# Hybrid mLSTM and convolution layer on Trainium2: readout joined to its gate, nine staging tiles for the w_out operands, and other slots at the start and the end

## Chip, core and metric

One core of one Trainium2 chip. The metric is the device time of one execution in microseconds: 1683.57 is the median of three runs of the kernel before (1682.82 to 1685.95).

## The reference

All in float32, 2048 tokens (S), width 1024.

```
h   = RMSNorm(x)                              # x: (2048, 1024)
P   = h @ w_in                                # 1024 x 8200: q k v o z_m i f | u B C z_c
y_m = silu(z_m) * sigmoid(o) * HeadNorm(mLSTM(q, k, v, i, f))   # 4 heads, dqk 128, dv 256
y_c = silu(z_c) * GroupNorm(B * causal_conv3(C * u))            # 16 groups of 64 channels
out = x + RMSNorm(concat(y_m, y_c) @ w_out)   # w_out: 2048 x 1024
```

The mLSTM is a chunkwise recurrence with a running-maximum stabiliser; in the kernel a chunk is 128 tokens and a group is two chunks of one head.

## The kernel before

**Products.** A matrix product of 256 by 1024 by 1024 (a *pair* of 128 columns each, times 1024 tokens) is done as seven products of quarters instead of eight (sums of quarters of both operands, a Winograd form). Each quarter product is 12 matmuls of 128x128 by 128x512, because each float32 operand is split into a high part and a rest (`split_h` on ScalarE, L190; `split_l` on VectorE, L193) and three of the four part products are kept (`mm_prod`, L309 to L311). The seven products use three PSUM banks in the order X D Y X Y D Y; `evac(j)` empties or copies a bank after product j, and TensorE may go on in that bank only then. The tile c that `evac(4)` makes (L532, VectorE) has to be done before product 6, the copy u of `evac(2)` (L527, ScalarE) before product 4.

**Passes and slots.** Pass 0 is the first 1024 tokens times w_in (32 pairs), pass 1 the second 1024 tokens (32 pairs); passes 2 and 3 are w_out (8 pairs each): first the half of its rows that takes y of the convolution, with the sums stored in DRAM (c_scr), then the half that takes the mLSTM's, added to them. One quarter product is one *slot*; U = 224 slots are a pass over w_in. Slots 0 to 13 are a start without the seven-product form (`start`), slots 14 to 27 do pairs 2 and 3 in turns (`two_pairs`); slot 224 begins pass 1, 448 pass 2, 504 pass 3. The order of everything is written out by hand: `on(slot, fn)` and `later(d, fn)` put work on an agenda, and `run_slot` emits a slot's entries in the order evacuations, weights, stores, all else. `in_order` then ties each engine to that order, SyncE included, which issues all DMAs. So an instruction that waits holds up everything behind it on its engine.

**Weights.** For the product of slot s, the loads are at s-8, the sums of quarters at s-5 (`w_sum`), the high part at s-4 and the rest at s-3.

**Operands of a pass.** Each of the seven operands (128 x 4 x 512) is loaded in two halves, m = 0 to 13 (`hop_fill`), into one of four staging tiles of 128x1024 (tags cv, cv, cu, rb, which other helpers use too), then split (`hop_high` at slot end-6+11m/14, `hop_low` a slot later) into tiles that the pass before has left product by product. The loads are put at end-10 for m < 4, and two slots after the staging tile's former user for the others.

**Pairs of a pass over w_in.** Pairs 0 to 7 give q, k and v, 8 to 23 the convolution, 24 to 31 the gates o and z_m (`take_oz`; `gate_oz`, L358 to L364, three slots after). `gate_oz` stores the gate to g_scr. The 32 groups of the mLSTM (`plan_group`) start every 10.4 slots in pass 0 and every 10.8 in pass 1, the last at slot 422, and store their readout h to h_scr at start+15. `o_make` (L1212) loads h and gate of one tile of 128 tokens, multiplies them, and stores to o_scr, where pass 3 reads: for the first 1024 tokens every 10 slots in pass 1, for the second every 4 slots from slot 452, in pass 2 and the first slots of pass 3.

**Start.** Squares of x, `inverse`, `diagonal` and `spread` give the norm's factors of one 512 tokens; `norm`, `diff` and `fill` make the operands of pass 0. v of head 0 is taken in slots 22 to 25 (`slow` in `plain_take`); its transpose on VectorE follows a slot later and four stores to v_scr of 64 KB each a slot after that.

**Pools.** Tag t5 has ten tiles of 128x512 for all that is short-lived; the mLSTM's tiles are in the pool `ml`, closed after pass 1, and the last pool, `op`, takes its place.

**End.** `row_take` adds c_scr's part to a tile of the result, squares it, and two slots after both halves of a row are there `row_out` scales it and adds x.

Of the kernel before, what the change touches and what calls it, by code (L numbers as in the profile page):

```python
# [9 lines left out]
F32 = mybir.dt.float32  # L10
F32R = mybir.dt.float32r
AF = mybir.ActivationFunctionType
ALU = mybir.AluOpType
# [52 lines left out]
def hybrid_layer_kernel(  # L66
# [39 lines left out]
    def scratch(name, shape):  # L106
        return [dram.tile(shape, F32, name=f"{name}{i}") for i in range(2)]

    y_scr = scratch("y_scr", [8, P, HT])
    h_scr = scratch("h_scr", [NH, NC, 2, P, P])  # L110
    g_scr = scratch("g_scr", [8, P, HT])
# [68 lines left out]
    def c4(tag, name, shape=None, dtype=F32):  # L180
        return cpool.tile(shape or [P, HT], dtype, tag=tag, name=name, bufs=2 if tag == "cv" else 1)
# [54 lines left out]

    def y_quarter(pas, t, half):

        src = (y_scr, o_scr)[pas][t // NC]
# [76 lines left out]
    def seg(qd):  # L316
        return slice(Q * qd, Q * qd + Q)
# [32 lines left out]
    def take_oz(hf, e, ch, qd, src, psum):  # L350
        if ch == 0:
            S["so", qd] = sigmoid(src)
        else:
            def go():
                S["z", qd] = (src, sigmoid(src))
            later(1, go)
            later(3, lambda: gate_oz(hf, e, qd))

    def gate_oz(hf, e, qd):
        so = S.pop(("so", qd))  # L360
        z, sz = S.pop(("z", qd))
        nc.vector.scalar_tensor_tensor(z, z, gh[:, e : e + 1], so, ALU.mult, ALU.mult)
        nc.vector.tensor_tensor(z, z, sz, ALU.mult)
        store(g_scr[hf][e][:, seg(qd)], z)  # L364

    def take_uc(hf, j, ch, qd, src, psum):
        if (ch, qd) == (0, 0):
# [77 lines left out]
    def gate_zz(hf, g, ch, qd, src, sg):  # L445
        cv = S["cv", ch][:, seg(qd)]
        nc.vector.tensor_tensor(sg, src, sg, ALU.mult)
        nc.vector.tensor_tensor(sg, sg, cv, ALU.mult)
        store(y_scr[hf][2 * g + ch][:, seg(qd)], sg)

    TAKE = {"qk": take_qk, "v": take_v, "oz": take_oz, "uc": take_uc, "bb": take_bb, "zz": take_zz}

# [7 lines left out]

    def row_take(n, ch, qd, src, psum):
        t = 2 * n + ch
        last = n == NOUT - 1 and ch == 0
        o = S["ot", t, qd] = op.tile([P, Q], F32, tag="ot", name="ot", bufs=4)
        nc.vector.tensor_tensor(o, src, S.pop(("pc", ch, qd)), ALU.add)

        def square():
            ss = op.tile([P, 1], F32, tag=f"oss{qd}", name="oss")
            nc.scalar.activation(t5("junk"), o, AF.Square, accum_out=ss)
            S.setdefault(("oss", t), []).append(ss)  # L470
            if len(S["oss", t]) == 1 + (n < NOUT - 1):
                S["xr", t] = op.tile([P, DM], F32, tag="xr", name="xr")
                nc.sync.dma_start(S["xr", t], x[t * P : (t + 1) * P, :])
            if len(S["oss", t]) == 2:
                row_rstd(t, last)

        def scale():
            nc.vector.tensor_tensor(o, o, S["gpost"][:, seg(qd)], ALU.mult)  # L478

        if last and qd == 1:  # L480
            square()
            scale()
        else:
            later(1, square)
            later(2, scale)

    def row_rstd(t, last):
        a, b = S.pop(("oss", t))
        nc.vector.tensor_tensor(a, a, b, ALU.add)
        rstd(a, 1.0 / DM)  # L490
        later(0 if last else 2, lambda: row_out(t, a, last))

    def row_out(t, r, last):
        xr = S.pop(("xr", t))
        for qd in range(2):
            o, dst = S.pop(("ot", t, qd)), out[t * P : (t + 1) * P, seg(qd)]
            nc.vector.scalar_tensor_tensor(o, o, r, xr[:, seg(qd)], ALU.mult, ALU.add)  # L497
            store(dst, o, 0 if last else 1)

    TAKE_OUT = (part_store, row_take)  # L500

# [404 lines left out]
    def hop_source(pas, j):  # L906

        if pas == 1:
            return hop_scr[j]
        half, ch = {0: (0, 0), 3: (1, 0), 6: (1, 1)}.get(j, (None, None))  # L910
        if half is None:
            return wo_scr[pas - 2][j]
        r = WOUT0[pas - 2] + half * KH * P
        return wout[r : r + KH * P, seg(ch)].rearrange("(e p) c -> p e c", p=P)

    def hop_fill(pas, m):

        j, half = divmod(m, 2)
        t = c4(STAGE[m % 4], "hst", [P, 2, Q])
        ks = slice(2 * half, 2 * half + 2)  # L920
        nc.sync.dma_start(t, hop_source(pas, j)[:, ks, :])
        return j, ks, t

    def hop_high(pas, m):
        j, ks, t = S["fill", pas, m]
        if m % 2 == 0:
            hops[pas, j] = (hop_tile(j, "H", f"hH{j}"), hop_tile(j, "L", f"hL{j}"))
        split_h(hops[pas, j][0][:, ks], t)

    def hop_low(pas, m):  # L930
        j, ks, t = S.pop(("fill", pas, m))
        H, L = hops[pas, j]
        split_l(H[:, ks], L[:, ks], t)


    def start():
# [110 lines left out]
        def plain_take(n, ch, qd, bank, t=None):  # L1047
            t = t or t5("u")
            nc.vector.tensor_tensor(t, bank, rb[:, seg(qd)], ALU.mult)
            kind, i = PAIRS[n]  # L1050
            slow = NSTART + 8 + 2 * ch + qd - clock[0] if kind == "v" else 0
            later(slow, lambda: TAKE[kind](0, i, ch, qd, t, False))

        load(0, 0)
        load_raw((0, 0, 0), wt[0, 0])
# [72 lines left out]

        p0 = [plain(0, 0, 1)]
        norm(2)  # L1130
        diagonal(1)
        fill(0, 0)
        run_slot()

        p0.append(plain(0, 1, 1))
        spread(1)
        fill(3, 2)
        spread_take(1)
        run_slot()

# [70 lines left out]

    def o_make(t, half):  # L1212

        hf, tt = divmod(t, NC)
        es, ts = slice(4 * half, 4 * half + 4), slice(tt * P, (tt + 1) * P)
        R = {}
        view = lambda a: a.rearrange("p (e t) -> p e t", t=P)

        def load():
            R["h"], R["g"] = t5("yh"), t5("yg")  # L1220
            for i in range(2):
                nc.sync.dma_start(
                    view(R["h"])[:, 2 * i : 2 * i + 2, :], h_scr[hf][2 * half + i, tt].rearrange("e p t -> p e t"))
            nc.sync.dma_start(view(R["g"]), g_scr[hf][es, :, ts].rearrange("e p t -> p e t"))

        def mult():
            nc.vector.tensor_tensor(R["h"], R["h"], R["g"], ALU.mult)
            store(o_scr[hf][es, :, ts].rearrange("e p t -> p e t"), view(R["h"]))

        return (0, load), (3, mult)  # L1230

# [13 lines left out]
    for i in range(NH * NG):  # L1245
        h, g = divmod(i, NG)
        plan_group(0, h, g, 47 + int(10.4 * i))
        plan_group(1, h, g, U + 36 + int(10.8 * i))
    for i in range(NC):
        on(60 + 10 * i, lambda i=i: norm_stat(i))  # L1250
    on(150, norm_fin)
# [1 line left out]
    for k in range(KH):  # L1253
        on(OZ0 + 10 + 9 * k, lambda k=k: hop_load(k))
        on(OZ0 + 15 + 9 * k, lambda k=k: hop_make(k))
        for p, s in enumerate((U + OZ0, 2 * U)):
            for d, fn in wo_make(p, k):
                on(s + 10 + 9 * k + d, fn)
    for i in range(2 * NT):
        for d, fn in o_make(*divmod(i, 2)):  # L1260
            on((U + 40 + 10 * i if i < NT else 2 * U + 4 + 4 * (i - NT)) + d, fn)

    def plan_fill(pas, end):
        for m in range(2 * NPROD):
            s = end - 6 + 11 * m // 14
            early = end - 10 if m < 4 else end - 6 + 11 * (m - 4) // 14 + 2
            def load(m=m):
                S["fill", pas, m] = hop_fill(pas, m)
            on(early, load)
            on(s, lambda m=m: hop_high(pas, m))  # L1270
            on(s + 1, lambda m=m: hop_low(pas, m))
# [7 lines left out]
        pair(0, n)  # L1279

    for n in range(NPAIR):
        pair(1, n)
# [4 lines left out]
    mlx.close()  # L1287


    op = ctx.enter_context(tc.tile_pool(name="op", bufs=2, reuse_waits="tile"))  # L1290
    S["gpost"] = op.tile([P, DM], F32, tag="gpost", name="gpost", bufs=1)
    nc.sync.dma_start(S["gpost"], g_post.broadcast_to([P, DM]))
# [4 lines left out]
    for pas in (2, 3):  # L1297
        for n in range(NOUT):
            pair(pas, n)
    while any(agenda.values()):  # L1300
        run_slot()

# [52 lines left out]
```

## Time and profile before

| | |
|---|---|
| median of 3 runs | 1683.57 us |
| the profiled execution | 1679.38 us, span 1677.6 us, mean granted clock 0.997 |
| TensorE, matmul | 1648.6 us busy, 98% |
| VectorE | 1276.7 us, 76% |
| ScalarE | 885.2 us, 53% |
| GpSimd | 129.5 us, 8% |
| DMA | 339 MB, 66.7% of 16 engines on SyncE's queue |

TensorE is busy throughout; the slices in which it is not are found from who waited for whom, and the instructions in order of time around the wait. Matmuls are pipelined: each is shown 0.39 us long, and they start every 0.227 us.

### The profile page before, as it was taken

The numbers are of one execution on the slowest core, as the hardware profiler recorded it, in microseconds if no ns is written. First come the engines' busy times: TensorE is split into PE (matmuls) and PEld (weight loads), VectorE is DVE, ScalarE is ACT, GpSimd is POOL, SyncE is SP. The second block draws the span as 40 slices with busy tenths as digits, with TensorE's granted clock in tenths as the row PEclk, the third lists the DMA queues.
The fourth block names the chain that finished last, engine by engine and source line by source line (L and its number), as shares of the span: only waits on it lengthen the run. The fifth ranks groups of instructions, "written<-read, shape, count | busy, mean of one in ns | idle before, by whom it ended". The sixth has DMA issues, their size and how long they took to land. (4 is left out here: it accounts for less than half of the span.)

```text
span 1677.6 us, 23360 instructions
## 1 busy us (share of the span) xinstructions
PE 1648.6 (98%) x7565; PEld 1366.9 (81%) x7565; DVE 1276.7 (76%) x2373; ACT 885.2 (53%) x1703; POOL 129.5 (8%) x142
## 2 busy tenths in 40 slices
PE   9999999999999999999999999999999999999997
PEld 7778888888888888788888888888888878887886
DVE  6987679898989788946557877786877586578886
ACT  6543456565656565634444556565565563355442
POOL 1000002010202001000000201010200000000111
PEclk9999999999999999999999999999999999999999
DMA  7378755564455688856885546455587688898764
GB/s 266 116 178 225 190 182 160 152 192 158 151 166 162 213 273 275 266 141 167 208 216 165 168 138 180 146 170 160 186 249 228 226 270 257 267 306 286 255 208 163
DMA packets 414539, 339.23 MB, mean 202 GB/s; under 512 B 191337, under 2 KB 306033, under 8 KB 414418
## 3 DMA queue, kind: packets, MB, share of 16 engines
q1 hardware_dynamic: 414418, 337.76, 66.7%
q8 instruction: 59, 0.97, 0.2%
q14 instruction: 62, 0.51, 0.1%
HBM read 218.90 MB, written 118.76 MB: 201 GB/s over the span
## 5 line engine op out<-in xcount | busy, mean ns | idle before, releaser
L190 ACT CAST w<-wraw 128x512 fp32r<-128x512 f32 x506 | 313.5, 621 | 292.0 <-PE uY L311 106.4
L193 DVE TENSOR_TENSOR w<-wraw,w 128x512 fp32r<-128x512 f32 x506 | 344.1, 684 | 104.5 <-ACT w L190 102.7
L309 PE MATMUL uY<-hH,w 128*128 128x512 f32 x936 | 368.3, 393 | 13.2 <-DVE c L532 6.3
L310 PE MATMUL uY<-hL,w 128*128 128x512 f32 x936 | 365.4, 390 | 0.0
L311 PE MATMUL uY<-hH,w 128*128 128x512 f32 x936 | 365.3, 390 | 0.0
L309 PE MATMUL uX<-hH,w 128*128 128x512 f32 x624 | 243.8, 391 | 2.2 <-ACT uY L521 2.2
L311 PE MATMUL uX<-hH,w 128*128 128x512 f32 x624 | 243.2, 390 | 1.6 <-DVE w L193 1.6
L309 PE MATMUL uD<-hH,w 128*128 128x512 f32 x624 | 244.6, 392 | 0.0
L311 PE MATMUL uD<-hH,w 128*128 128x512 f32 x624 | 243.2, 390 | 0.0
L310 PE MATMUL uD<-hL,w 128*128 128x512 f32 x624 | 243.0, 389 | 0.0
L310 PE MATMUL uX<-hL,w 128*128 128x512 f32 x624 | 242.9, 389 | 0.0
L309 PEld LDWEIGHTS uY<-hH,w 128*128 128x128 f32 x936 | 176.1, 188 | 52.7 <-DVE c L532 6.5
L311 PEld LDWEIGHTS uY<-hH,w 128*128 128x128 f32 x936 | 176.1, 188 | 37.5
L310 PEld LDWEIGHTS uY<-hL,w 128*128 128x128 f32 x936 | 176.3, 188 | 35.1 <-DVE hL L193 0.5
L309 PEld LDWEIGHTS uX<-hH,w 128*128 128x128 f32 x624 | 117.2, 188 | 26.8 <-ACT uY L521 3.0
L311 PEld LDWEIGHTS uX<-hH,w 128*128 128x128 f32 x624 | 117.1, 188 | 26.7 <-DVE w L193 2.0
L311 PEld LDWEIGHTS uD<-hH,w 128*128 128x128 f32 x624 | 117.1, 188 | 24.8
L310 PEld LDWEIGHTS uX<-hL,w 128*128 128x128 f32 x624 | 117.2, 188 | 23.7
L309 PEld LDWEIGHTS uD<-hH,w 128*128 128x128 f32 x624 | 117.2, 188 | 23.5
L310 PEld LDWEIGHTS uD<-hL,w 128*128 128x128 f32 x624 | 117.3, 188 | 23.3
L532 DVE TENSOR_TENSOR c<-p,uY 128x512 f32<-128x512 f32 x78 | 53.3, 684 | 86.3 <-PE uY L311 83.5
L527 ACT COPY u<-uY 128x512 f32<-128x512 f32 x78 | 45.6, 585 | 94.1 <-PE uY L311 92.8
(201 smaller groups left out, 2221.9 us busy)
## 6 DMA issues: line engine op xcount, KB each, us to landing
wraw<-in_wt_dram SPq DMA_DIRECT2D x226, 256.0 KB
wraw<-w_scr SPq DMA_DIRECT2D x120, 256.0 KB
w_scr<-wraw SPq DMA_DIRECT2D x90, 256.0 KB
v_scr<-tr SPq DMA_DIRECT2D x128, 64.0 KB
vraw<-v_scr SPq DMA_DIRECT2D x32, 256.0 KB
h_scr<-hT SPq DMA_DIRECT2D x128, 64.0 KB
y_scr<-sg SPq DMA_DIRECT2D x32, 256.0 KB
g_scr<-c SPq DMA_DIRECT2D x32, 256.0 KB
```

Source lines behind the costliest of these rows:

```text
L190: nc.scalar.copy(dH, src)
L193: nc.vector.tensor_tensor(dL, src, dH.bitcast(F32), ALU.subtract)
L309: nc.tensor.matmul(bank, wH[:, k, :], bH[:, k, :], start=first, stop=False, **kw)
L310: nc.tensor.matmul(bank, wH[:, k, :], bL[:, k, :], start=False, stop=False, **kw)
L311: nc.tensor.matmul(bank, wL[:, k, :], bH[:, k, :], start=False, stop=stop and k == KH - 1, **kw)
L527: nc.scalar.copy(sb["u"], bank["Y"])
L532: nc.vector.tensor_tensor(c, sb["p"], bank["Y"], ALU.add)
```

## The change

1. **Readout and gate joined for the second 1024 tokens.** `take_oz` loads the readout h from h_scr a slot after the take, and `gate_oz`, now four slots after the take, multiplies it in as a third operation and stores the product straight to o_scr. `o_make` is left for the first 1024 tokens alone, every 8 slots.
2. **Nine staging tiles for passes 2 and 3.** The pool `ml` is closed before pair 31 of pass 1, and a pool `stage` with five tiles of 128x1024 opens in its place. Loads m = 4 to 8 go to it at end-7 to end-5, m = 9 to 12 to the first four tiles at end-4 to end-2, and m = 13 goes to two tiles of t5 at end+1. `stage` closes at product 4 of pass 3, where `op` opens.
3. **y of the convolution by tiles.** y_scr is laid out so that a load of one quarter (128 x 4 x 128) is contiguous, 2 KB a partition, and the stores are in pieces of 512 B; before, the stores were contiguous and the loads in pieces of 512 B.
4. **Start.** `fill(0, 0)` and `fill(3, 2)` go ahead of `diagonal(1)`; v of head 0 is taken in slots 16, 19, 21 and 23, and the second half of k of head 0 in slot 15 instead of at once.
5. **Groups of the mLSTM** start every 10 slots or a little more, so that start modulo 7 is neither 1 nor 3: the last of pass 1 starts at slot 418 instead of 422.
6. **End.** The last pair's rows are squared and scaled at once, the odd row is finished ahead of the even one, the sum of a row's two squares moves from VectorE to GpSimd, and x is loaded a slot earlier.

```diff
-    y_scr = scratch("y_scr", [8, P, HT])
+    y_scr = scratch("y_scr", [NC, 2, P, 4, P])
...
-            later(3, lambda: gate_oz(hf, e, qd))
+            if hf == 0:
+                later(3, lambda: gate_oz(hf, e, qd))
+            else:
+                later(1, lambda: readout_load(e, qd))
+                later(4, lambda: gate_oz(hf, e, qd))
+
+    def readout_load(e, qd):
+        t = S["h", qd] = t5("yh")
+        h, dv = divmod(e, 2)
+        nc.sync.dma_start(
+            t.rearrange("p (c t) -> p c t", t=P),
+            h_scr[1][h, 4 * qd : 4 * qd + 4, dv].rearrange("c p t -> p c t"))
...
-        store(g_scr[hf][e][:, seg(qd)], z)
+        if hf:
+            nc.vector.tensor_tensor(z, z, S.pop(("h", qd)), ALU.mult)
+        store((g_scr, o_scr[1])[hf][e][:, seg(qd)], z)
...
-        store(y_scr[hf][2 * g + ch][:, seg(qd)], sg)
+        half, e = divmod(2 * g + ch, 4)
+        store(
+            y_scr[hf][4 * qd : 4 * qd + 4, half, :, e, :].rearrange("c p t -> p c t"),
+            sg.rearrange("p (c t) -> p c t", t=P))
...
+        end = n == NOUT - 1
...
+        square()
+        if full:
+            row_rstd(t)
+        scale()
+        if (ch, qd) == (0, 1):
+            row_out(t + 1)
+            row_out(t)
...
-        nc.vector.tensor_tensor(a, a, b, ALU.add)
+        nc.gpsimd.tensor_tensor(a, a, b, ALU.add)
...
-        t = c4(STAGE[m % 4], "hst", [P, 2, Q])
+        i = m % (4 if pas == 1 else 9)
...
+        if m == 13 and pas > 1:
+            parts = [(slice(k, k + 1), t5("hst")[:, None, :]) for k in (2, 3)]
+        elif i < 4:
+            parts = [(ks, c4(STAGE[i], "hst", [P, 2, Q]))]
+        else:
+            parts = [(ks, S["stage"].tile([P, 2, Q], F32, tag=f"st{i}", name="hst"))]
...
-            slow = NSTART + 8 + 2 * ch + qd - clock[0] if kind == "v" else 0
-            later(slow, lambda: TAKE[kind](0, i, ch, qd, t, False))
+            slot = {("v", 0, 0): 16, ("v", 0, 1): 19, ("v", 1, 0): 21, ("v", 1, 1): 23, ("qk", 1, 1): 15}
+            later(slot.get((kind, ch, qd), clock[0]) - clock[0], lambda: TAKE[kind](0, i, ch, qd, t, False))
...
         norm(2)
-        diagonal(1)
         fill(0, 0)
         run_slot()
 
         p0.append(plain(0, 1, 1))
+        fill(3, 2)
+        diagonal(1)
         spread(1)
-        fill(3, 2)
         spread_take(1)
...
+    for hf, first in enumerate((47, U + 36)):
+        s = first - 10
+        for i in range(NH * NG):
+            s += 10
+            while s % NPROD in (1, 3):
+                s += 1
+            plan_group(hf, *divmod(i, NG), s)
...
-    for i in range(2 * NT):
+    for i in range(2 * NC):
         for d, fn in o_make(*divmod(i, 2)):
-            on((U + 40 + 10 * i if i < NT else 2 * U + 4 + 4 * (i - NT)) + d, fn)
+            on(U + 40 + 8 * i + d, fn)
...
-            early = end - 10 if m < 4 else end - 6 + 11 * (m - 4) // 14 + 2
+            n = 4 if pas == 1 else 9
+            if m == 13 and pas > 1:
+                early = end + 1
+            elif m >= n:
+                early = end - 6 + 11 * (m - n) // 14 + 2
+            elif m < 4:
+                early = end - 11 + m // 2
+            else:
+                early = end - 7 + (m - 4) // 2
```

## Rows read from the trace of the kernel before

**Rows 1.** Waits of TensorE, 55 to 130 us: total us, times, longest

```profile
PE uY L309 <- DVE c L532: 3.0, 1, 3.0
PE uX L309 <- ACT uY L521: 2.2, 2, 1.5
PE uX L311 <- DVE w L193: 1.6, 1, 1.6
PE uY L309 <- ACT uY L521: 0.8, 1, 0.8
```

**Rows 2.** Waits of TensorE, 250 to 690 us (two rows), 720 to 1300 us (two rows)

```profile
PE uY L309 <- DVE c L532: 1.6, 1, 1.6
PE uY L309 <- ACT uY L521: 0.4, 1, 0.4
...
PE uY L309 <- ACT uY L521: 0.7, 1, 0.7
PE num L701 <- DVE pL L193: 0.7, 1, 0.7
```

**Rows 3.** TensorE in order of time: start, us, instruction, [idle before, releaser]

```profile
1351.23 0.39 PE L309 MATMUL uY<-hH,w 128*128 128x512 f32 x1
1353.95 0.39 PE L309 MATMUL uX<-hH,w 128*128 128x512 f32 x1
...
1366.70 0.50 PE L309 MATMUL uY<-hH,w 128*128 128x512 f32 x1 [1.71 <-ACT u L527]
1372.79 0.47 PE L309 MATMUL uY<-hH,w 128*128 128x512 f32 x1 [0.36 <-DVE c L532]
...
1523.34 0.79 PE L309 MATMUL uY<-hH,w 128*128 128x512 f32 x1 [3.27 <-ACT u L527]
1526.80 0.40 PE L311 MATMUL uY<-hH,w 128*128 128x512 f32 x1
...
1550.28 0.50 PE L309 MATMUL uY<-hH,w 128*128 128x512 f32 x1 [0.60 <-DVE c L532]
```

**Rows 4.** The start in order of time, VectorE, ScalarE and SyncE's queue

```profile
47.42 0.57 ACT L997 COPY rb<-ssq 128x512 f32<-128x512 f32 x1
49.84 5.39 DVE L1002 SCALAR_TENSOR_TENSOR xs<-xs,gp,rb 128x512 f32<-128x512 f32 x8
58.61 0.71 DVE L329 STREAM_TRANSPOSE tr<-u 128x512 f32<-128x512 f32 x1
...
110.48 5.68 SPq L214 DMA_DIRECT2D v_scr<-tr  x8
```

**Rows 5.** Waits of VectorE, 40 to 126 us

```profile
DVE s L251 <- DMA wraw<-in_wt_dram: 5.6, 1, 5.6
```

**Rows 6.** VectorE in order of time, ahead of slot 448

```profile
1338.97 0.69 DVE L193 TENSOR_TENSOR w<-wraw,w 128x512 fp32r<-128x512 f32 x1 [0.64 <-ACT w L190]
...
1342.19 0.74 DVE L362 SCALAR_TENSOR_TENSOR c<-c,gh,sg 128x512 f32<-128x512 f32 x1
...
1348.99 0.68 DVE L532 TENSOR_TENSOR c<-p,uY 128x512 f32<-128x512 f32 x1
```

**Rows 7.** Waits of VectorE, 1337 to 1374 us

```profile
DVE hL L193 <- ACT hH L190: 1.9, 3, 1.3
```

**Rows 8.** Waits of ScalarE, 1497 to 1528 us

```profile
ACT hH L190 <- DMA hst<-wo_scr: 7.1, 5, 4.1
```

**Rows 9.** The end in order of time, VectorE and GpSimd

```profile
1667.61 0.69 DVE L465 TENSOR_TENSOR ot<-uY,pc 128x512 f32<-128x512 f32 x1 [0.63 <-PE uY L311]
1671.82 0.93 POOL L426 TENSOR_TENSOR oss<-oss,mhalf 128x1 f32<-128x1 f32 x1
1673.04 1.41 DVE L497 SCALAR_TENSOR_TENSOR ot<-ot,oss,xr 128x512 f32<-128x512 f32 x2
```

**Rows 10.** One item of o_make after slot 452: its last load, its product

```profile
1368.57 0.47 SPq L1224 DMA_DIRECT2D yg<-g_scr  x1
1376.15 0.68 DVE L1227 TENSOR_TENSOR yh<-yh,yg 128x512 f32<-128x512 f32 x1
```

More of the change, by code (lines that the diff above doesn't have):

```diff
@@ L107, in scratch @@
         return [dram.tile(shape, F32, name=f"{name}{i}") for i in range(2)]
-    y_scr = scratch("y_scr", [8, P, HT])
+    y_scr = scratch("y_scr", [NC, 2, P, 4, P])
     h_scr = scratch("h_scr", [NH, NC, 2, P, P])
-    g_scr = scratch("g_scr", [8, P, HT])
+    g_scr = dram.tile([8, P, HT], F32, name="g_scr")
     graw_scr = scratch("graw_scr", [4, NH, HT])
@@ L237, in y_quarter @@
     def y_quarter(pas, t, half):
-        src = (y_scr, o_scr)[pas][t // NC]
+        if pas == 0:
+            return y_scr[t // NC][t % NC, half]
+        src = o_scr[t // NC]
         return src[4 * half : 4 * half + 4, :, t % NC * P : (t % NC + 1) * P].rearrange("e p t -> p e t")
@@ L462, in row_take @@
         t = 2 * n + ch
-        last = n == NOUT - 1 and ch == 0
+        end = n == NOUT - 1
         o = S["ot", t, qd] = op.tile([P, Q], F32, tag="ot", name="ot", bufs=4)
         nc.vector.tensor_tensor(o, src, S.pop(("pc", ch, qd)), ALU.add)
+        full = ("oss", t) in S
+        if not full:
+            S["oss", t] = op.tile([P, 2], F32, tag="oss", name="oss", bufs=4)
+        ss = S["oss", t][:, qd : qd + 1]
+        if full != end:
+            S["xr", t] = op.tile([P, DM], F32, tag="xr", name="xr")
+            nc.sync.dma_start(S["xr", t], x[t * P : (t + 1) * P, :])
@@ L467, in square @@
         def square():
-            ss = op.tile([P, 1], F32, tag=f"oss{qd}", name="oss")
             nc.scalar.activation(t5("junk"), o, AF.Square, accum_out=ss)
[L470 to L475, printed above, removed]
         def scale():
@@ L478, in scale @@
             nc.vector.tensor_tensor(o, o, S["gpost"][:, seg(qd)], ALU.mult)
[L480 to L483, printed above, removed]
+        if not end:
             later(1, square)
             later(2, scale)
-    def row_rstd(t, last):
-        a, b = S.pop(("oss", t))
-        nc.vector.tensor_tensor(a, a, b, ALU.add)
+            if full:
+                later(1, lambda: row_rstd(t))
+                later(3, lambda: row_out(t))
+            return
+        square()
@@ L490, in row_rstd, with row_out @@
+        if full:
+            row_rstd(t)
[3 more added lines that the diff above has]
+            row_out(t)
+    def row_rstd(t):
+        a, b = (S["oss", t][:, qd : qd + 1] for qd in range(2))
+        nc.gpsimd.tensor_tensor(a, a, b, ALU.add)
         rstd(a, 1.0 / DM)
[L491 to L495, printed above, removed]
+    def row_out(t):
+        xr, r = S.pop(("xr", t)), S.pop(("oss", t))[:, 0:1]
+        for qd in (1, 0):
@@ L496, in row_out @@
             o, dst = S.pop(("ot", t, qd)), out[t * P : (t + 1) * P, seg(qd)]
             nc.vector.scalar_tensor_tensor(o, o, r, xr[:, seg(qd)], ALU.mult, ALU.add)
-            store(dst, o, 0 if last else 1)
+            store(dst, o, 0 if t >= NT - 2 else 1)
     TAKE_OUT = (part_store, row_take)
@@ L918, in hop_fill @@
         j, half = divmod(m, 2)
-        t = c4(STAGE[m % 4], "hst", [P, 2, Q])
+        i = m % (4 if pas == 1 else 9)
         ks = slice(2 * half, 2 * half + 2)
-        nc.sync.dma_start(t, hop_source(pas, j)[:, ks, :])
-        return j, ks, t
+        if m == 13 and pas > 1:
[4 more added lines that the diff above has]
+            parts = [(ks, S["stage"].tile([P, 2, Q], F32, tag=f"st{i}", name="hst"))]
+        for ks, t in parts:
+            nc.sync.dma_start(t, hop_source(pas, j)[:, ks, :])
+        return j, parts
     def hop_high(pas, m):
-        j, ks, t = S["fill", pas, m]
+        j, parts = S["fill", pas, m]
         if m % 2 == 0:
             hops[pas, j] = (hop_tile(j, "H", f"hH{j}"), hop_tile(j, "L", f"hL{j}"))
-        split_h(hops[pas, j][0][:, ks], t)
+        for ks, t in parts:
+            split_h(hops[pas, j][0][:, ks], t)
     def hop_low(pas, m):
-        j, ks, t = S.pop(("fill", pas, m))
+        j, parts = S.pop(("fill", pas, m))
         H, L = hops[pas, j]
-        split_l(H[:, ks], L[:, ks], t)
+        for ks, t in parts:
+            split_l(H[:, ks], L[:, ks], t)
     def start():
@@ L1212, in o_make @@
     def o_make(t, half):
-        hf, tt = divmod(t, NC)
-        es, ts = slice(4 * half, 4 * half + 4), slice(tt * P, (tt + 1) * P)
+        es, ts = slice(4 * half, 4 * half + 4), slice(t * P, (t + 1) * P)
         R = {}
@@ L1222, in load @@
                 nc.sync.dma_start(
-                    view(R["h"])[:, 2 * i : 2 * i + 2, :], h_scr[hf][2 * half + i, tt].rearrange("e p t -> p e t"))
-            nc.sync.dma_start(view(R["g"]), g_scr[hf][es, :, ts].rearrange("e p t -> p e t"))
+                    view(R["h"])[:, 2 * i : 2 * i + 2, :], h_scr[0][2 * half + i, t].rearrange("e p t -> p e t"))
+            nc.sync.dma_start(view(R["g"]), g_scr[es, :, ts].rearrange("e p t -> p e t"))
         def mult():
             nc.vector.tensor_tensor(R["h"], R["h"], R["g"], ALU.mult)
-            store(o_scr[hf][es, :, ts].rearrange("e p t -> p e t"), view(R["h"]))
+            store(o_scr[0][es, :, ts].rearrange("e p t -> p e t"), view(R["h"]))
         return (0, load), (3, mult)
@@ L1244, in hybrid_layer_kernel @@
     plan_gates(1, U + 9, False)
[L1245 to L1248, printed above, removed]
+    for hf, first in enumerate((47, U + 36)):
[5 more added lines that the diff above has]
+            plan_group(hf, *divmod(i, NG), s)
     for i in range(NC):
@@ L1281, in hybrid_layer_kernel @@
     for n in range(NPAIR):
+        if n == NPAIR - 1:
+            mlx.close()
+            stx = ExitStack()
+            S["stage"] = stx.enter_context(tc.tile_pool(name="stage", bufs=1, reuse_waits="tile"))
         pair(1, n)
@@ L1286, in hybrid_layer_kernel @@
                 later(0, lambda qd=qd, bank=bank: gate_take(1, qd, bank))
[L1287 to L1292, printed above, removed]
     for n in range(NOUT):
@@ L1296, in hybrid_layer_kernel @@
             on(s + d, lambda n=n, ch=ch, qd=qd: part_load(n, ch, qd))
-    for pas in (2, 3):
-        for n in range(NOUT):
-            pair(pas, n)
+    for n in range(NOUT):
+        pair(2, n)
+    step = products(3, 0, bank_)
+    for j in range(NPROD):
+        if j == 4:
+            stx.close()
+            op = ctx.enter_context(tc.tile_pool(name="op", bufs=2, reuse_waits="tile"))
+            S["gpost"] = op.tile([P, DM], F32, tag="gpost", name="gpost", bufs=1)
+            nc.sync.dma_start(S["gpost"], g_post.broadcast_to([P, DM]))
+        step(j)
+    for n in range(1, NOUT):
+        pair(3, n)
     while any(agenda.values()):
```

## The prediction, on record before the changed kernel ran

> **What bounds the kernel now.** I read the busy table first, then TensorE's waits, then the instructions around each. TensorE is busy nearly all the time, and the change adds and removes no matmul, so only its stops and what follows the last matmul can move. From product to product the start moves by 2.72 us for 12 matmuls [rows 3], 0.227 us each. A stop costs about 0.27 us more than the idle shown: a matmul is drawn 0.39 us long, 0.16 over its pitch, and the first after a stop takes 0.11 longer. The stops are in five places:
>
> - the start: 3.0 + 2.2 + 1.6 + 0.8 = 7.6 us in five stops [rows 1], with 5 x 0.27 about 8.9;
> - the middle of passes 0 and 1: 1.6 + 0.4 + 0.7 + 0.7 in four [rows 2], about 4.5;
> - around slot 448: 1.71 and 0.36 [rows 3], about 2.6;
> - around slot 504: 3.27, then 8 pitches that take 3.46 us in place of 1.81 (1523.34 to 1526.80), then 0.60 [rows 3]: 3.43 + 1.65 + 0.87 = 5.9;
> - the end: VectorE's last operations finish 1673.04 + 1.41, some 6.9 us after the last product's bank is read at 1667.61 [rows 9].
>
> The reader is to see in rows 5 to 8 that each of these waits for VectorE or ScalarE, and that behind these stands a DMA that SyncE issued late, or VectorE's own queue.
>
> **Start, two effects.** First, `fill(0, 0)` and `fill(3, 2)` now precede the diagonal, for which ScalarE waits. Their VectorE halves then run before the factors rb are there; so `norm(1)` can start when rb is copied, at 47.42 + 0.57 = 48.0, instead of 49.84: 1.8 us. One transpose of k (0.71 in the row, some 0.65 from start to start) [rows 4] leaves the chain as well. VectorE is thus 2.4 us earlier at the first stop, which removes it (1.6 + 0.27), and leaves 0.5 for the next two. The moved transposes (k at slot 16, v at 17, 20, 22, 24 for 23 to 26) come back behind these, but their number is the same by slot 27. I take 2.4 us, between 0.7 (the transpose alone) and 4.8 (all three stops of 2.2 and 1.6).
>
> Second, the stop of 3.0: VectorE waits 5.6 us for weights [rows 5], whose load stands in SyncE's queue behind eight v_scr stores that take 5.68 us [rows 4], 0.71 each. Four of the eight are v of head 0, which now go several slots earlier: 4 x 0.71 = 2.8 us, of the 3.27 that the stop costs. Below nothing is possible if the same stores in slots 18 to 25 delay weights there; the loads are issued eight slots ahead, so I take 2.8, from 0 to 3.3. The start together: **-5.2**.
>
> **Middle.** The group's starts move by up to four slots. The stops there are single meetings of a group's operations with the convolution's, with `gate_oz` or with the sums for pass 1, on VectorE or ScalarE. Where `hop_make` (slots 183 to 186) met the transposes of a readout at 185, these now fall on 187: I count the stop of 1.6 as gone (1.9 with its share) and the three small ones as replaced by others. **-1.9**, between -4.5 and +2 (as many new ones as there were, half the size). Around slot 224 the loads keep their four tiles and nearly their slots: 0.
>
> **Slot 448.** Here the change works in both directions. Nine tiles bring the loads m = 4 to 12 three to four slots forward, so ScalarE no longer waits for them. But VectorE is nearly full, and its order is by slots: between 1337 and 1374 it waits only 1.9 us, three times [rows 7]. The change makes each `gate_oz` longer by one operation of 0.68 [rows 10], 1.4 to 2.1 us from start to start, and puts it one slot later. The two gates of pair 30 were in slots 442 and 443 and are in 443 and 444. The first one used to fill time in which VectorE waits for a cast of ScalarE anyway (the wait that ends at 1338.97); now nothing does. From 1342.19, the start of a gate, to c of pair 31 at 1348.99 [rows 6] there was one gate of 1.4 us, and there will be two of 2.1: c starts at 1348.99 + 0.7 + 2.1 = 1351.8 and ends at 1352.5, and product 6 wants its bank at 1351.23 [rows 3]. A new stop of 1.3 us. From this c to the next, the one that released 1372.79, are 1372.79 - 0.1 - 0.7 - 1348.99 = 23.0 us, with two more gates in it (+1.4) and 1.6 us of the waits of rows 7, which go: 22.8. So the next c starts at 1374.6 and ends at 1375.3; TensorE, 1.3 late, would be there at 1352.55 + 7 x 2.72 = 1371.6: a stop of 3.7. Further, at slot 450 eight t5 tiles are held by pair 31's gates (two readouts among them) and two by m = 13: ScalarE's copy p needs an eleventh, and waits until a gate of VectorE's slot 450 has read its tiles, with the copy u and two casts behind it. These come 1.2 us too late for VectorE; I add 1.0. Together 1.3 + 3.7 + 1.0 = 6.0 in place of 2.6, and with the share of one stop more 6.3: **+3.7**. From below -2.2 (no stop but 0.4, if the loads were all that was missing), from above +6.
>
> What the row at 1523.34 shows bears on this: after the idle of 3.27 us the matmuls start every 0.43 us for a while, 1.2 GHz, and 1.65 us are lost; after 3.0 [rows 1] nothing of the kind is listed, 2.4 GHz throughout. The new stop lies between and beyond. The Trainium skill, "TensorE: Matmul & The Clock Gate", section "Part 1: The HAM clock gate (the "warmup" mystery)", says that the array passes to half its clock once it has been idle long enough and returns after sustained work. By that rule a stop of 3.7 would cost 1.65 us more, and the sum would be -8.1 instead of -9.8; my stop is split by ScalarE's and VectorE's waits, so I leave it out and let the range hold it.
>
> **Slot 504.** ScalarE waits 7.1 us for DMAs of staging tiles, 4.1 at once [rows 8]. There the 16 items of `o_make` for the second 1024 tokens go (48 loads and 16 stores; 16 stores and 16 loads of the gate disappear altogether, 32 x 256 KB), their products too, and the loads come three to four slots earlier. VectorE has room there: by slots it has 2 to 3.8 us of work per 2.72, without gates. x a slot earlier serves the stop at 1550.28. I take 5.4 of 5.9 as gone: **-5.4**, from -5.9 to -2.5 (the clock's share and the last stop alone).
>
> **The y layout** swaps pieces of 512 B and 2 KB between 32 stores and 32 loads of the same size: nothing; both are issued a pass and more ahead of any need.
>
> **End.** After the last bank is read at 1667.61, VectorE used to do one scaling and two outputs behind GpSimd's power (1671.82 + 0.93) [rows 9]. The odd row's outputs now go before, so the even row waits for GpSimd alone: square and its sum done at about 1669.2, then three operations on GpSimd, 0.93 each at most: 1669.2 + 2.8 = 1672.0, against 1673.04: **-1.0**, from -1.5 to +0.5 (if GpSimd is still at the odd row).
>
> **Sum.** -5.2 - 1.9 + 0 + 3.7 - 5.4 - 1.0 = -9.8. The profiled execution, 1679.4 (1.8 over its span), becomes 1669.6. The runs' median is 4.2 above the profiled execution, so the forecast is 1683.6 - 9.8 = **1673.8**, with a range of its own of 1669 to 1679.
>
> **Rivals.**
> - *The tiles relieve slot 448 too.* For it: the stop at 1366.70 is released by ScalarE, which had waited for staging loads. Against: VectorE's waits there are only 1.9. Then -2.2 in place of +3.7: 1667.9. Chance 0.15.
> - *The start does not improve.* VectorE is the bound there, the same work is only permuted, and the stores of v jam SyncE some slots earlier. Then -1 for -5.2, and nothing from the middle: -9.8 + 4.2 + 1.9 = -3.7, 1679.9. For it: the stops of 2.2 wait behind VectorE. Against: the idle that the diagonal made is real. Chance 0.18.
> - *Slower: the readouts land late.* In pass 1 each gate waits in VectorE's order for a load issued three slots (8.2 us) before. In the eight pairs, if the load landed x later than 8.2, VectorE would stand x twice a pair, the second mostly inside the first. It has spare time and two slots until c, some 3 us; beyond, every us costs 8. To be slower by 0.2% than before needs 9.8 + 3.4 = 13.2, or 1.7 a pair: from a landing of 12.9 us on; at 13.0 us, 1688. The nearest row: three loads, the last issued at 1368.57, were used at 1376.15 [rows 10], so they landed within 7.6. Chance 0.06.
> - *The change does not do what it says:* `stage` takes the place of tiles still in use, and its loads wait. The last group's stores are at slot 433, the first such load at 441, so this needs 8 slots of delay. It would take the early loads away at slot 448: 1675 to 1678. Chance 0.03.
>
> **How the numbers follow.** The forecast with its own range has 0.58. Two executions of this kernel can be told apart from about 0.2% on, 3.4 us: faster is below 1680.2. That holds the forecast, the first rival, the last, and half of the second: 0.58 + 0.15 + 0.03 + 0.09, less some for the forecast's upper end, 0.82. Within 0.2% are the other half of the second and some of that end: 0.11. Slower 0.07. The range, 1667.5 to 1681.5, reaches to the first rival and over the second and leaves the slow one out.
>
> **What would show it.** Right: no stop near 61 us and a short one or none near 121; new waits of TensorE for c ahead of slot 448 and a longer one at about 17 us after it; none over 1 us around slot 504, granted clock 1.00 there; VectorE's last operation about 1 us nearer to the last matmul. Wrong: no stop on c at the end of pair 31 (then the gates' third operation is hidden); ScalarE still waiting for staging tiles at slot 504; gates in pass 1 that wait for yh; stops in the middle that add to more than 4.

## The result: 0.7% faster, and the profile after

The median after is 1672.11 us (1670.52 to 1673.61, four runs), beside 1683.19 before (1682.11 to 1685.95, four runs): a ratio of 0.9933, 95% interval 0.9917 to 0.9949. The forecast was 1673.8, in a range of 1667.5 to 1681.5. The profiled execution took 1672.65 us (span 1670.9) in place of 1679.38 (1677.6). So the traces differ by 6.7 us, the medians by 11.1; that gap is explained below.

The page of the kernel after, busy times and DMA: TensorE does what it did, and 8 MB less is moved.

```profile
span 1670.9 us, 23313 instructions
PE 1648.9 (99%) x7565; PEld 1368.0 (82%) x7565; DVE 1277.6 (76%) x2359; ACT 882.6 (53%) x1705; POOL 132.4 (8%) x158
DMA packets 397419, 330.84 MB, mean 198 GB/s; under 512 B 190601, under 2 KB 288913, under 8 KB 397298
```

The best account is by the start of one and the same product in both traces, since all else follows TensorE. After minus before, in us:

| stretch | slots | forecast | measured |
|---|---|---|---|
| start | to 36 | -5.2 | -2.0 |
| middle | 36 to 446 | -1.9 | +0.4 (-0.9 to slot 222, +1.7 from 222 to 234, -0.5 in pass 1) |
| pass 2 begins | 446 to 458 | +3.7 | +2.1 |
| pass 3 begins | 497 to 520 | -5.4 | -6.1 |
| end | last matmul to the span's end | -1.0 | -1.1 |
| sum | | -9.8 | -6.7 |

TensorE after, in order of time (start, us, instruction, idle before and releaser); these answer to [rows 1] and [rows 3]:

```profile
71.35 0.50 PE L311 MATMUL uX<-hH,w 128*128 128x512 f32 x1 [0.69 <-ACT uY L546]
84.72 0.80 PE L311 MATMUL uY<-hH,w 128*128 128x512 f32 x1 [2.19 <-ACT u L552]
85.31 0.63 PE L312 MATMUL uY<-hL,w 128*128 128x512 f32 x1
...
87.45 0.63 PE L311 MATMUL uY<-hH,w 128*128 128x512 f32 x1
...
95.73 0.50 PE L311 MATMUL uY<-hH,w 128*128 128x512 f32 x1 [1.05 <-ACT u L552]
...
1350.97 0.50 PE L311 MATMUL uY<-hH,w 128*128 128x512 f32 x1 [1.17 <-DVE c L557]
...
1366.43 0.50 PE L311 MATMUL uY<-hH,w 128*128 128x512 f32 x1 [1.57 <-ACT u L552]
...
1373.45 0.47 PE L311 MATMUL uY<-hH,w 128*128 128x512 f32 x1 [1.26 <-DVE c L557]
```

The stops near 61 and 121 us are gone, as said. Two others are there instead, at 84.72 and 95.73, and after the first the matmuls start 0.43 us apart (85.31 to 87.45 is five of them), 1.2 GHz; the granted clock between 84 and 88 us is 0.57. Ahead of slot 448 stands the stop on c (1.17; forecast 1.3). Around slot 504 TensorE waits for nothing.

The other engines after, in order of time, answer to [rows 4] to [rows 6] and [rows 9]:

```profile
84.08 0.58 ACT L552 COPY u<-uY 128x512 f32<-128x512 f32 x1 [2.03 <-DVE tr L331]
...
109.23 2.17 SPq L214 DMA_DIRECT2D v_scr<-tr  x4
115.69 0.69 DVE L253 TENSOR_TENSOR s<-wraw 128x512 f32<-128x512 f32 x1 [1.48 <-DMA wraw<-in_wt_dram]
...
1340.60 0.74 DVE L375 SCALAR_TENSOR_TENSOR c<-c,gh,sg 128x512 f32<-128x512 f32 x1
1342.10 0.69 DVE L378 TENSOR_TENSOR c<-c,yh 128x512 f32<-128x512 f32 x1
1345.05 0.74 DVE L375 SCALAR_TENSOR_TENSOR c<-c,gh,sg 128x512 f32<-128x512 f32 x1
1350.23 0.68 DVE L557 TENSOR_TENSOR c<-p,uY 128x512 f32<-128x512 f32 x1
1363.84 0.59 ACT L549 COPY p<-uD 128x512 f32<-128x512 f32 x1 [4.09 <-DVE c L375]
1372.62 0.68 DVE L557 TENSOR_TENSOR c<-p,uY 128x512 f32<-128x512 f32 x1
...
1662.32 0.68 DVE L483 TENSOR_TENSOR ot<-uY,pc 128x512 f32<-128x512 f32 x1
1665.34 0.93 POOL L441 TENSOR_TENSOR oss<-oss,mhalf 128x1 f32<-128x1 f32 x1
1666.30 1.41 DVE L522 SCALAR_TENSOR_TENSOR ot<-ot,oss,xr 128x512 f32<-128x512 f32 x2 [0.44 <-POOL oss L441]
```

The reader is to see four things. Of the eight v_scr stores in a row four are left (109.23), and VectorE's wait for weights behind them is 1.48 instead of 5.6. The new stop at 84 stands behind a transpose: ScalarE's copy u waited 2.03 us for VectorE. Ahead of slot 448 two gates now have a third operation, and behind it the copy p waits 4.09 us for a gate of the last pair. At the end the even row waits 0.44 for GpSimd alone.

Stretches (columns: start and end, length, busy us of PE, PEld, DVE, ACT, POOL, then granted clock, DMA share, GB/s), 1370 to 1480 and 1475 to 1535 us, first before, then after, and after also 84 to 88 us:

```profile
1370.00:1480.00 110.00, 109.64 (x483) 90.31 (x482) 67.63 (x105) 39.94 (x71) 0.00 (x0) 1.00 0.86 268
1475.00:1535.00 60.00, 56.73 (x243) 46.49 (x242) 45.42 (x62) 33.42 (x52) 0.00 (x0) 0.97 0.96 311
```

```profile
1370.00:1480.00 110.00, 108.74 (x480) 89.79 (x479) 62.39 (x97) 38.54 (x69) 0.00 (x0) 1.00 0.62 199
1475.00:1535.00 60.00, 60.00 (x267) 49.67 (x266) 46.63 (x65) 36.17 (x60) 2.89 (x6) 1.00 0.83 277
84.00:88.00 4.00, 3.28 (x8) 2.60 (x9) 2.98 (x5) 2.05 (x3) 0.00 (x0) 0.57 0.26 31
```

With the transfers of `o_make` out of pass 2 the DMA engines have room (0.62 for 0.86, and 0.83 for 0.96 where TensorE had stopped).

### The profile page after: what moved, and what is told of

Read it like the earlier page. It is cut to its first block, busy times and chain, and to the rows that moved or that the text cites. A ratio compares the mean times of both kernels' runs of the same rounds, so it can differ in the third digit from the quotient of the medians.

```text
span 1670.9 us, 23313 instructions
## 1 busy us (share of the span) xinstructions
PE 1648.9 (99%) x7565; PEld 1368.0 (82%) x7565; DVE 1277.6 (76%) x2359; ACT 882.6 (53%) x1705; POOL 132.4 (8%) x158
## 4 chain that ended last, share of the span: by engine, by line
PE 85%; DVE 7%; DMA 3%; ACT 2%; issue 2%; SPq 1%; DVEq 0%; POOL 0%; POOLq 0%; ACTq 0%
PE uY L311 11%; PE uY L313 11%; PE uY L312 11%; PE uX L311 7%; PE uX L313 7%; PE uX L312 7%; PE uD L313 7%; PE uD L312 7%; PE uD L311 7%; DVE hL L193 1%; DVE w L193 1%; PE num L724 1%; PE num L725 1%; PE num L726 1%; PE gate L598 1%
## 5 line engine op out<-in xcount | busy, mean ns | idle before, releaser
L546 ACT COPY uY<-uX 128x512 f32<-128x512 f32 x78 | 44.6, 571 | 109.3 <-PE uX L313 109.1
```

Of the source, the lines that this page charges most:

```text
L546: nc.scalar.copy(bank["Y"], bank["X"])
```

## Experiments

**1. The parts alone.** Four kernels, each the kernel before with one part of the change: the start (part 4), the joined readout (part 1), the nine tiles (part 2), and the rest (parts 3, 5 and 6).

```diff
 # start_only: before, with
-        diagonal(1)
         fill(0, 0)
...
+        fill(3, 2)
+        diagonal(1)
         spread(1)
-        fill(3, 2)
 # and the table of slots for v and k of head 0
 # join_only: before, with readout_load, the third product, the store to o_scr, o_make for 1024 tokens
 # tiles_only: before, with the pool stage, hop_fill in nine tiles and their slots
 # rest_only: before, with y_scr by tiles, the groups' starts, the end
```

> The kernel before with the change's start alone (the fills ahead of the diagonal, other slots for v and k of head 0). Theory: what the start gives is decided by VectorE's queue and by t5 tiles that it frees late; the stop near 61 us goes, one near 82 us comes for the copy u, and slot 40 is reached 2.0 us earlier than before, as in the changed kernel's trace; the rest is the kernel before: -2.0 us, stops around slots 448 and 504 2.6 and 5.9. Rival: the start gives the -5.2 of the forecast in most executions, and the profiled one of the changed kernel was an unlucky one: -4 to -6 us.

> The kernel before with readout and gate joined, nothing else. Theory: VectorE's third operation makes a stop of 1.2 to 1.4 us on c in slot 447, and the stops around slot 448 add to 5 or more in place of 2.6, since the four staging tiles make ScalarE wait as well; around slot 504 the transfers and products of o_make are gone, which takes 3 of the 5.9 us: in all about -1 us. Rival, that slot 504 stops for want of staging tiles: it stays over 4 us there, and the kernel is 1 to 3 us slower than before.

> The kernel before with nine staging tiles for passes 2 and 3, nothing else. Theory: VectorE is what bounds slot 448, so that the stops there fall from 2.6 only to 1 to 1.5; around slot 504 the loads come early and ScalarE waits no more than 1 us, but o_make's operations stay on VectorE: 1 to 2 in place of 5.9: in all -5 us. Rival, DMA volume: the engines are at 1.0 around slot 504, early loads only move the jam, and 3 or more of 5.9 stay: -2 to -3 us.

> The kernel before with the change's other parts: y by tiles, the groups' new starts, and the end. Theory: the end gives -1.2, the new starts move stops about, -0.7 in pass 0, +1.6 around slot 224 (the last group of pass 0 ends two slots later) and +0.8 in pass 1, y by tiles nothing: +0.5 us in all. Rival: the new starts are what the larger part of the 11 us comes from in most executions: -3 or better.

Measured, beside 1682.17 for the kernel before; the last two columns are us gained (-) or lost against its trace in the two stretches of slots:

| kernel | median | ratio, 95% | 446 to 458 | 497 to 520 |
|---|---|---|---|---|
| start_only | 1678.51 | 0.9975 (0.9966, 0.9984) | -0.4 | +0.7 |
| join_only | 1682.76 | 1.0004 (0.9995, 1.0014) | +5.9 | -4.4 |
| tiles_only | 1682.08 | 0.9996 (0.9986, 1.0006) | -2.2 | +1.8 |
| rest_only | 1678.46 | 0.9974 (0.9964, 0.9985) | -0.4 | -1.6 |
| all | 1672.11 | 0.9933 (0.9917, 0.9949) | +2.1 | -6.1 |

Three of the four theories missed by their numbers, and the start's -3.7 lies between its theory and its rival. The join was to give -1 us and gave +0.6; the tiles were to give -5 and gave -0.1, for the rival's reason, the DMA engines; the rest was to give +0.5 and gave -3.7, which is its rival's figure. The trace of the rest is 3.2 us late at slot 36, by the stop near 121 us that is taken up below; after it, it gains 1.7 up to slot 446, 0.4 and 1.6 in the two stretches and 1.2 at the end. Only those 1.2 can be put down to one of its three parts; y by tiles and the groups' starts were not run alone.

Join and tiles do nothing by themselves, each for a reason that the other takes away. TensorE with the join alone:

```profile
1357.58 0.50 PE L309 MATMUL uY<-hH,w 128*128 128x512 f32 x1 [1.18 <-DVE c L545]
1366.66 0.50 PE L309 MATMUL uY<-hH,w 128*128 128x512 f32 x1 [0.59 <-ACT uY L534]
1375.49 0.80 PE L309 MATMUL uY<-hH,w 128*128 128x512 f32 x1 [3.10 <-ACT u L540]
1376.09 0.63 PE L310 MATMUL uY<-hL,w 128*128 128x512 f32 x1
```

The gates' third operation makes the same stop of 1.18, and the loads, still in four tiles, one of 3.10 with a fall of the clock behind it (ScalarE waits 9.4 us for staging tiles between 1350 and 1377 us). With the tiles alone TensorE has at slot 448 only a stop of 0.34, but at slot 504

```profile
1532.16 0.77 PE L309 MATMUL uY<-hH,w 128*128 128x512 f32 x1 [4.68 <-DVE c L532]
1532.72 0.63 PE L310 MATMUL uY<-hL,w 128*128 128x512 f32 x1
```

and behind it VectorE (waits, 1500 to 1533 us) and the DMA engines (the stretch 1475 to 1535 us; share 1.00, 328 GB/s):

```profile
DVE ot L465 <- DMA pc<-c_scr: 4.1, 1, 4.1
DVE yh L1236 <- DMA yg<-g_scr: 0.9, 1, 0.9
```

```profile
1475.00:1535.00 60.00, 55.31 (x239) 45.44 (x238) 44.11 (x60) 33.25 (x52) 0.00 (x0) 0.98 1.00 328
```

Loads put earlier into engines that were already at 0.96 only push another load (c_scr's part) late. The medians of the parts add to -3.7 + 0.6 - 0.1 - 3.7 = -6.9, the whole is -11.1. The 4 us between them lie within the noise of five medians, and by the ratios they are 2.7. That the parts help each other is shown by the traces, at these two places: the parts add to +2.9 and -3.5, the whole is +2.1 and -6.1.

**2. The two halves of the start.** Kernel before, with the order of `fill` and `diagonal` alone, and with the slots of v and k alone.

```diff
 # slots_only
-            slow = NSTART + 8 + 2 * ch + qd - clock[0] if kind == "v" else 0
+            slot = {("v", 0, 0): 16, ("v", 0, 1): 19, ("v", 1, 0): 21, ("v", 1, 1): 23, ("qk", 1, 1): 15}
```

> The kernel before with the fills of the start ahead of the diagonal, old slots for v and k. Theory: the stop near 61 us is gone or under 0.3, slot 16 comes 2.0 to 2.5 us earlier, and that stays to slot 28; the stop near 121 us stays (3.2 to 4.5 us and, where longer than 3.2, 1.65 of low clock): -2 us. Rival, only slots matter: what is won at 61 is lost at the next two stops, 0.

> The kernel before with the new slots for v and k of head 0 alone, diagonal ahead as before. Theory (four of the eight v_scr stores leave SyncE's queue ahead of the weights): the stop near 121 us falls from 3.2 to 4.5 us and the low clock to under 0.5; new stops for u near 83 us cost 2 to 4 with the clock: -1 to -3 us. Rival, VectorE decides alone at 121: its idle for weights stays over 4 us, and the stop over 2.

The order alone takes 1680.85, the slots alone 1681.67, beside 1683.70 for the kernel before: ratios 0.9983 (0.9974 to 0.9993) and 0.9983 (0.9973 to 0.9993). VectorE's wait between 100 and 126 us, order alone:

```profile
DVE s L251 <- DMA wraw<-in_wt_dram: 5.5, 1, 5.5
```

With the slots alone that wait is not listed, and the stop near 121 is gone; but TensorE and ScalarE have the new ones:

```profile
86.20 0.59 ACT L527 COPY u<-uY 128x512 f32<-128x512 f32 x1 [2.03 <-DVE tr L329]
...
97.87 0.50 PE L309 MATMUL uY<-hH,w 128*128 128x512 f32 x1 [2.58 <-ACT u L527]
```

So the order takes the stop at 61 away, the slots the one at 121, and the slots bring those at 84 and 95. With the order alone no stop lies between 73 and 108 us.

**3. Where slot 448 loses.** Two kernels from the one after: the third product on GpSimd, a slot later, with the gate back at +3; and the load m = 13 of pass 2 in a staging tile instead of two t5.

```diff
 # a_gps3
+            nc.gpsimd.tensor_tensor(z, z, r, ALU.mult)
+            store(o_scr[1][e][:, seg(qd)], z)
+        later(1, join)
 # a_m13
-        if m == 13 and pas > 1:
+        if m == 13 and pas > 2:
```

> The changed kernel with the gate's two operations back at three slots after the take and the third, the product with the readout, on GpSimd a slot later. Theory (VectorE's queue makes the stops around slot 448): the stop on c in slot 447 (1.17 us idle in the changed kernel) goes, of the two after slot 448 (1.57 and 1.26) at most one of 0.6 stays, 448 costs under 1.2 in place of 4.8: about -3.5 us against the changed kernel, -14 against the kernel before. Rival: GpSimd's product of 128x512 takes 2 us or more and holds t5 tiles and the stores, or slows VectorE beside it: no gain, stops on p and u stay: -11 against before.

> The changed kernel with load m = 13 of pass 2 in a staging tile in place of two t5 tiles. Theory (ten t5 tiles are one too few at slot 450): ScalarE's copy p no longer waits 4.1 us for the gate, the stop on u (1.57) goes; but VectorE is full there, so that the stop on c behind it grows from 1.26 to 1.8 or 2.3: -0.5 to -1 us in all. Rival, that the t5 tile is the whole cause after slot 448: both stops go, -2.8 us. Other rival: p waits as before for another tile, nothing moves.

GpSimd: 1672.35, ratio to before 0.9930 (0.9915 to 0.9945), as the kernel after: the rival's figure, not the theory's. The stop of 1.17 is gone, and others are there. TensorE, then VectorE and GpSimd:

```profile
1367.72 0.50 PE L312 MATMUL uD<-hL,w 128*128 128x512 f32 x1 [1.26 <-DVE hL L193]
1371.47 0.77 PE L311 MATMUL uY<-hH,w 128*128 128x512 f32 x1 [2.31 <-DVE c L563]
```

```profile
1341.22 1.62 POOL L383 TENSOR_TENSOR c<-c,yh 128x512 f32<-128x512 f32 x1 [4.34 <-DVE c L376]
1341.61 1.78 DVE L253 TENSOR_TENSOR s<-wraw 128x512 f32<-128x512 f32 x1
```

The sum of 0.68 us on VectorE takes 1.78 while GpSimd multiplies for 1.62: here moving 0.69 us off VectorE cost it 1.1. The Trainium skill, "GPSIMD Engine Reference", section "8. Key points", says that the two share their ways into SBUF and hinder each other where a VectorE instruction has two inputs there; these rows agree, and give it a size.

The staging tile: 1673.98, 0.9940 (0.9925 to 0.9955). I had forecast a gain; the median is 1.9 above that of the kernel after, with intervals that overlap, and the trace loses 2.7 more between slots 446 and 458. The wait of p is gone (it starts at 1357.99), and TensorE stands as long, in one piece:

```profile
1349.26 0.50 PE L311 MATMUL uY<-hH,w 128*128 128x512 f32 x1 [1.18 <-DVE c L557]
1371.74 0.76 PE L311 MATMUL uY<-hH,w 128*128 128x512 f32 x1 [3.10 <-DVE c L557]
1372.31 0.63 PE L312 MATMUL uY<-hL,w 128*128 128x512 f32 x1
```

Up to its first matmul a stop costs 0.16 more than its idle: 3.26 here, 1.73 + 1.42 = 3.15 after. What sets both is VectorE between one c and the next, 22.39 us in either kernel, of which it works (the stretch between, VectorE alone, of the kernel after)

```profile
1350.92:1372.62 21.70, 21.53 (x27) 1.00 0.54 169
```

all but 0.2 us, while TensorE wants it after 7 x 2.72 = 19.0. So the t5 tile was late, and cost nothing of its own: p's wait only moved half of the stop to an earlier place. It even saved something, since after 1.57 and 1.26 us the clock stayed at 2.4 GHz, while after 3.10 it fell for thirteen matmuls and took another 2.6.

**4. Fewer gates ahead of slot 448.** From the kernel after: join only six of the eight pairs; the gates of the last two are stored, and multiplied in pass 2, from slot 462 on.

```diff
-            if hf == 0:
+            if hf == 0 or e >= 6:
...
-        if hf:
+        if hf and e < 6:
...
+    for i in range(4):
+        for d, fn in late_join(6 + i // 2, i % 2):
+            on(2 * U + 14 + 6 * i + d, fn)
```

The second kernel also changes the start again: k of head 0 at once, v in slots 18, 20, 22 and 24. The kernel after ran beside them.

> The changed kernel once more, unaltered, beside the kernel before. The trace before and the trace after differ by 6.7 us, the medians by 11.1. Theory: the profiled execution of the kernel before was one of those in which the stop near 121 us stays just too short for the low clock (3.05 us idle); three other profiles with the same start lost 1.8 to 4.2 us more by slot 36. Then the ratio repeats at 0.993 to 0.994, and this second profile lies within 2 us of the first, start included (slot 36 within 0.3). Rival: the changed kernel varies as much as the one before, its first runs were lucky, and the ratio is 0.995 or more.

> The changed kernel with gate and readout joined for the first six of eight pairs only; the last two store the gate, and four loads of gate and readout with a product each follow in pass 2, from slot 462. Theory (VectorE's third operations and the moved gates around slot 448 are what the joining costs): no stop in slot 447, at most 1 us after slot 448, 0.5 to 1.0 in place of 4.7: -4 us against the changed kernel, -15 against the kernel before. Rival: loads m = 13 and the casts on ScalarE stop it as well, 2 or more of the 4.7 stay; or the four late products make stops in pass 2: less than 2 us gained.

> The same with k of head 0 taken at once and v in slots 18, 20, 22 and 24. Theory (t5 tiles held by k and early transposes on VectorE make the new stops near 82 and 94 us): they fall from 2.2 and 1.0 to under 1 together, and the stop near 121 us stays under 1: -1.5 to -3 us against the other start. Rival, VectorE's work up to slot 27 is the same and its queue full: the same 2 to 4 us are lost a few slots later, 0.

| kernel | median (range) | ratio to before, 95% |
|---|---|---|
| after, again | 1671.40 (1671.08 to 1672.39) | 0.9933 (0.9919, 0.9947) |
| late_join | 1666.64 (1666.36 to 1667.82) | 0.9905 (0.9891, 0.9918) |
| late_join_s2 | 1665.32 (1664.78 to 1665.48) | 0.9895 (0.9882, 0.9909) |

With late_join c to c is 20.95 us, and TensorE's only stop at slot 448 is

```profile
1368.59 0.47 PE L312 MATMUL uY<-hH,w 128*128 128x512 f32 x1 [0.32 <-DVE c L572]
```

From c to c VectorE has the same instructions as in the kernel after but for two multiplications of 0.69 (22.39 - 20.95 = 1.44; tiles_only, whose gates have no third operation either, has 20.94), and ahead of the first c two more are gone. That is worth 4.8 us by the medians, and 4.3 in the traces between slots 446 and 458. So the two stops after slot 448 were the third operation of the gates. For the stop ahead of it one thing is not separated: late_join, like a_gps3, which has no stop there either, also puts these gates a slot earlier again. Both kernels beat the one before and the one after. The second one's start has shorter stops (1.27 near 84 us, none near 95, 1.45 near 121, no fall of the clock), and slot 36 is at -3.5 us where the kernel after has -2.0. Its median is 1.3 us below that of late_join, a little less than the 1.5 to 3 expected, and its stops near 84 and 121 us are longer than the 1 us that was expected at most.

## Why the prediction was right, and where it was not

**Slot 448: mechanism right, one term too many.** Forecast: c of pair 31 starts at 1351.8; TensorE was 1.6 early by then, so 1350.2; it started at 1350.23. From c to c 22.8 was said, 22.39 measured. The 1.0 us added for the late t5 tile was the step that failed: the tile was late as described, by 4.09 us, but a_m13 shows that it lies beside VectorE's own lateness and does not come on top. That and the 0.4 from c to c make most of the difference between +3.7 and +2.1. The clock's share, left out because the stop would be split, did stay away: the granted clock is 1.00 between 1366 and 1380 us, and a_m13, with the stop in one piece, has the fall. The rival that the tiles relieve this place too has fallen for this kernel; tiles_only shows that it holds where the gates stay short.

**Slot 504: right**, -6.1 for -5.4. Both stops and the low clock between them are gone, and the granted clock is 1.00. I credited the early loads and the missing transfers together; the missing transfers alone give 4.4 (join_only), the early loads alone lose 1.8 (tiles_only).

**Start: -2.0 for -5.2.** What was said to go went: the product of slot 16 starts 2.6 us earlier (2.4 forecast), and between slots 28 and 36 another 4.5 are gained, the stop of 3.05 and one of 0.83. Of the other two a stop of 1.50 went and one of 0.68 stayed. But between slots 20 and 28 5.1 us are lost. The step that failed is that the moved transposes "come back behind these" without a price. Taken earlier, v and k hold t5 tiles while their transposes stand in VectorE's queue, and ScalarE's copies, p and u, wait for a tile: 2.35 and 1.21 us lost at 84.72 and 95.73, and 1.5 for eight matmuls at 1.2 GHz. These 1.5 are no loss of their own. In a_gps3, whose start is the same, the clock stayed high, the second stop was the longer for it, and slot 36 came at -1.9:

```profile
95.80 0.50 PE L311 MATMUL uY<-hH,w 128*128 128x512 f32 x1 [2.58 <-ACT u L558]
```

slots_only shows that it is these slots; the shares of k and of v are not separated. The second rival, that the start does not improve, was half right: VectorE's queue is the bound there, but the start did improve.

**Middle: +0.4 for -1.9.** The stop of 1.6 fell to 0.38 at 579.38, near as said. Around slot 224, counted as nothing, 1.7 were lost. They vary between executions: against the same profile of before, the traces with the code of the kernel after lose 0.8 to 1.7 there, those whose code is still that of the kernel before 0.0 to 1.3, and tiles_only, where only two loads lie otherwise, a slot earlier, 2.3. What sets them stays open.

**End: -1.1 for -1.0.**

**The y layout** was put at nothing because its transfers stand "a pass and more" ahead of any need. That is too much: its last store starts at 1199.7 us, its loads at 1326.6 to 1473.0, less than half a pass behind. No engine waits for one of these loads in the kernel after, but the layout was not run alone.

**The total was closer than its terms.** By the traces the change was forecast at -9.8 and is -6.7. The forecast of 1673.8 added 4.2 to the profile for the distance of the median. For the kernel before it held; the kernel after has its median 0.5 below its profile. These two errors cancel to 1.7, which is luck. The reason for the 4.2 lies at 121 us. In before's profile the stop there was 3.05 us and the clock stayed high [rows 1]. Four kernels with before's slots for v had there 3.28 (order_only), 3.33 (tiles_only), 4.02 (rest_only) and 4.32 (join_only), each followed by matmuls 0.43 apart; tiles_only, rest_only and join_only, the same up to that place, were 1.8, 3.2 and 4.2 us later at slot 36 than before's profile:

```profile
124.92 0.50 PE L309 MATMUL uY<-hH,w 128*128 128x512 f32 x1 [3.05 <-DVE c L532]
124.92:128.92 4.00, 3.99 (x18) 1.00 0.95 271
...
123.74 0.50 PE L309 MATMUL uY<-hH,w 128*128 128x512 f32 x1 [3.28 <-DVE c L532]
123.74:127.74 4.00, 4.00 (x12) 0.63 0.98 276
```

The first two lines are of before, the last two of order_only; the second of each is the stretch behind the stop, TensorE alone, with its granted clock (1.00 and 0.63). So that profile was a lucky one: its 1679.38 lies below all 63 other runs of the kernel before, the fastest of which took 1679.83. The removed stop is worth more in the median: start_only gains 1.95 in its trace up to slot 36, and 3.7 by the medians. How often the runs without a profile have the fall at this place is not shown.

**The slower rival** needed gates that stand at least 1.7 us a pair for their readout. One of the sixteen third products waited for it, 1.22 us, and TensorE's stop behind it was 0.40 (at 1271.41):

```profile
1266.74 0.69 DVE L378 TENSOR_TENSOR c<-c,yh 128x512 f32<-128x512 f32 x1 [1.22 <-DMA yh<-h_scr]
```

The last rival, that the pool's early loads wait for tiles still in use, is refuted by the order of transfers: the last group's stores start by 1313.1 us, the first of these loads is issued at 1334.42, and between 1335 and 1362 us ScalarE waits for no staging load, where it waited 3.4 us before.

## What to carry to other kernels

Where one engine is busy 98% of the time, list its stops and ask of each which in-order queue ends last; a late tile beside a fuller engine cost nothing here, and removing it gained nothing. Two parts that each measure as nothing (1.0004 and 0.9996) may be two halves of a gain, when each uncovers what the other removes; look in the trace for where each lost what it won. An operation joined to another at a boundary between passes is cheap in bytes and dear on the engine that is full just there: leave it joined elsewhere, and do the last few later.

## What the hardware showed

- A stop's length alone did not decide whether the clock fell. The stop near 84 us was followed by a fall after idles of 2.19 us (after), 2.17 (after_again) and 2.19 (start_only; granted clock 0.57 from 84 to 88 us in the first, 0.63 and 0.57 from 85 to 89 in the others), and by none after 2.15 (a_gps3), 2.19 (a_m13) and 2.20 (late_join; granted clock 1.00 in all three). Near 95 us it fell after 2.57 in late_join, and not after 2.58 in a_gps3; near 121 us it fell after 3.28 (order_only), and not after 3.05 (before). A fall took 1.5 us (after, eight matmuls) to 2.6 (a_m13, thirteen). The Trainium skill, "TensorE: Matmul & The Clock Gate", section "Why this matters for your kernels", advises against long idle gaps between bursts of matmuls if the clock is to stay up; these rows agree that the falls follow gaps, and show gaps of one length with either outcome.
- A GpSimd product of 128x512 took 1.28 to 1.74 us (a_gps3, sixteen of them) where VectorE takes 0.69, and a VectorE sum beside one of 1.62 took 1.78 instead of 0.68.
